# A hybrid attention step: a third score bank in turn, the first chunk in halves, and small pieces of work moved between engines

## The chip, the cores and the metric

The kernel runs on one core of a Trainium2 chip. TensorE (PE) multiplies, VectorE (DVE), ScalarE (ACT) and GpSimd (POOL) do the rest, and SyncE (SP) issues most transfers; each engine works through its own instructions in order. The metric is the time of one execution in microseconds (us).

## What is computed

One layer of a diffusion backbone on 128 context ("prompt") tokens and 1024 latent tokens, D = 1024. Cut to what matters:

```python
shift, scale, gate = split(silu(cond) @ w_mod + b_mod)
h = rmsnorm(x, norm_gain) * (1 + scale) + shift
q_a, k_a, v_a, g_a, q_b, k_b, v_b, g_b = split(h @ w_in)     # 8 heads and 2 kv heads of 64 in a and in b
q, k = rmsnorm(q), rmsnorm(k)                                # latent tokens: then a rotation by position
o_a = softmax(q_a k_a^T / 8) v_a                             # all latent keys and the cached context keys
o_b = softmax([sink, q_b k_b^T / 8]) v_b                     # keys within 128 positions, and the context keys
y = x + gate * (concat(o_a * silu(g_a), o_b * silu(g_b)) @ w_out)
```

The prompt attends to itself alone, and its keys and values are returned too.

## The kernel before

A float32 product is made of three products of rounded parts (high by high, low by high, high by low), so most operands exist twice, as a rounded "high" copy and a "low" rest. The rounded copies are casts, mostly on ScalarE; the rests are subtractions on VectorE or GpSimd. The kernel has these stages, and at the end of the program `in_order` fixes each engine's instructions to the order in which the Python code emitted them:

1. **Start and first gates** (0 to 66 us in the profile). Tokens come in nine tiles of 128 rows; tiles 1 to 8 are latent, tile 0 is the prompt. For each tile `squares` (L380 to L384) makes the inverse root mean square with ScalarE and GpSimd, `scaled` (L387) applies it on VectorE, `turned_tile` (L397) transposes the tile on TensorE in two banks (`px`, four 128x128 pieces each), and `keep` (L401) copies each bank into `xT`. For each chunk j of 128 model columns `modulate_rows` (L353) multiplies the conditioning with the scale and shift columns of `w_mod` (tile `wm`, loaded for j = 0 in two halves), a copy (L356, `mrows`), `modulate` (L362 to L368) turns that into columns `a_mod` and `b_col`, and `modulated` (L410 to L412) makes `h` (high on ScalarE, `hf` on VectorE, low on GpSimd). Then a loop over j multiplies chunk j-1 of `h` with the gate weights `W_GA` for tiles 1 to 4 (`pg_f`, L266 to L271, 512 columns), and chunk j-2 for tiles 5 and 6 (`pg_s`, 256 columns). `warm(n)` (L431) issues n products of the identity with itself into an unused bank; their result is never read.
2. **Queries, keys, values, second gates** (66 to 299 us). In the second gates the first output weights `wo` are split into high and low too (`split_wo`, L1043 and L1044).
3. **Attention and output** (299 us to the end). A unit i is (tile t, branch m, kv head g): i = 0 is tile 1, branch a, head 0; i = 1 the same in branch b; i = 2 branch a, head 1; and so on; units 32 to 35 are the prompt's. Every unit has *slots*, one for each block of 128 keys: nine in branch a, three or four in branch b. In a slot of branch a TensorE makes the scores `st` (L1170, L1171, two banks "B"), ScalarE their exponential `pe` (L1173) and its rounded copy `ph` (L1177), GpSimd the rest `pl` (L1181; block 4's on VectorE, L1179), and three slots later TensorE multiplies both with the values (`pv`, L1191 to L1194, two banks "C"). In branch b the scores `sn` (L944, L945) lie in banks "A" and are made while the branch-a unit before still runs, in its slots 0 to 3; VectorE masks them (L948), ScalarE makes the exponential `pen` (L934), and in the unit's own slots TensorE transposes it (L1165). The maxima of a later branch-a unit (`pmx` on TensorE, L889, `mx` on VectorE, L890) use banks "A" as well. When a unit's last values are done, `inverse` (L1203, or L1205 and L1206), `gated` (L1215, L1217) and `parts` (L1227, L1229) follow after `END_AT` = 1, 4, 6 slots, and after 9 its output products `po` (L1262) join a queue from which `OUTRATE` = 2.5 or `PADRATE` = 3 a slot are taken. The last five pieces of `wo` are loaded and split inside this stage: `WO_LATE` gives the slot of each load, the split comes three slots later.

The order in a slot is: what `tick` has due (casts, exponentials `pen`, subtractions), the scores, the loads, the maxima and branch-b scores, output products, and the values of three slots ago.

```python
BANKS = {"A": 2, "B": 2, "C": 2, "D": 1, "E": 1}
WO_LATE = {12: 13, 13: 20, 11: 27, 14: 29, 15: 31}
```

Bank "E" is used by transposes before the attention stage and by the output products there; the first of these take it after slot 24.

Of the kernel before, what the change touches and what calls it, by code (L numbers as in the profile page):

```python
# [115 lines left out]
def hybrid_step(ctx, tc, x_prompt, x_sample, cache_k_a, cache_v_a, cache_k_b, cache_v_b,  # L116
                cols, w_mod_ss, w_mod_g, b_mod, w_in, qn_a, kn_a, qn_b, kn_b, sink_b, w_out,
                k_ident, k_cos, k_sin, k_mask,
# [200 lines left out]
    with tc.tile_pool(name="st", bufs=2, side="right") as st:  # L319
        ident = st.tile([P, P], F32, name="ident", bufs=1)  # L320
        nc.sync.dma_start(ident, k_ident)
# [27 lines left out]
        def modulate_rows(j):  # L349
            pm = pmod[j] = bank_tr(f"pm{j}")  # L350
            for k in range(KT):
                a = 32 * (k % 4)
                nc.tensor.matmul(pm[a : a + 32, 0:256], sil32[:, k, :], wm[j][:, k].rearrange("p s n -> p (s n)"),  # L353
                                 start=(k < 4), stop=(k >= 4), tile_position=(0, a))
# [1 line left out]
            (nc.scalar.copy if j > 1 else nc.vector.tensor_copy)(mrows[j], pm[:, 0:256])  # L356
# [29 lines left out]
        def scaled(t):  # L386
            nc.vector.tensor_scalar(xn[t], xn[t], rx.pop(t), None, op0=ALU.mult)  # L387

        def turned_tile(t, tags, between=None):

            for c in range(2):
                if c and between:
                    between()
                px[t, c] = bank(tags[c], f"px{t}_{c}")
                for i in range(4):
                    k = 4 * c + i
                    nc.tensor.transpose(px[t, c][:, P * i : P * i + P], xn[t][:, P * k : P * k + P], ident)  # L397
# [5 lines left out]
        def modulated(j, t0, n, cond):  # L403
# [6 lines left out]
            nc.scalar.activation(h_at(0, i, j, to), xT[:, j, dst], AF.Identity, scale=a, bias=b)  # L410
# [998 lines left out]
```

## Time and profile before

| | us |
|---|---|
| median of 3 runs (lowest, highest) | 704.11 (703.66, 704.31) |
| the profiled execution | 703.62 |
| its span in the profile | 701.4 |
| busy in the span: PE, DVE, ACT, POOL | 690.6, 462.5, 419.2, 337.9 |

The profile is one execution. Its span runs from the first to the last instruction that was recorded; some 2 us lie around it. Rows of the timeline and of the chain of waits give the start in us from the span's start, the length, the engine, the line, and what is written and read. Matmuls overlap: a 128x512 one shows about 0.39 us, but the next starts 0.23 us after it. So two starts, not a length, tell what a product costs.

### The profile page before, as it was taken

How to read it: one execution, taken by the hardware profiler on the slowest of the kernel's cores; microseconds unless marked ns; L12 is line 12 of the kernel's file. 1: busy time of each engine (PE TensorE's matmuls, PEld its weight loads, DVE VectorE, ACT ScalarE, POOL GpSimd, SP SyncE). 2: the span in 40 equal slices, each digit the busy share in tenths (PEclk: the TensorE clock that was granted, in tenths of full speed). 3: DMA queues.
4: the chain of work that ended last, by engine and by line, in shares of the span. 5: the costliest groups of instructions: out<-in, count | busy, mean ns of one | idle time of the engine just before them, and what ended most of it. 6: DMA issues, size and time to landing. Idle time of an engine off the chain costs nothing.

```text
span 701.4 us, 10680 instructions
## 1 busy us (share of the span) xinstructions
PE 690.6 (98%) x3532; PEld 559.5 (80%) x3532; DVE 462.5 (66%) x998; ACT 419.2 (60%) x858; POOL 337.9 (48%) x358
## 2 busy tenths in 40 slices
PE   7999999999999999999999999999999999999997
PEld 4778988878788889986788787788887888887876
DVE  4667257968768854676667567567676775775563
ACT  6646411422313423399877887787788778877870
POOL 3547024233313321267676654765575557455752
PEclk9999999999999999999999999999999999999999
DMA  8962283349344016332222121122221221212324
GB/s 319 412 214 111 78 306 75 91 131 279 87 124 132 16 61 209 129 84 77 75 83 89 47 83 54 62 67 75 69 75 40 68 91 46 82 54 91 92 75 128
DMA packets 53703, 78.57 MB, mean 112 GB/s; under 512 B 7112, under 2 KB 25864, under 8 KB 52752
## 3 DMA queue, kind: packets, MB, share of 16 engines
q1 hardware_dynamic: 45952, 66.74, 28.9%
q10 hardware_dynamic: 7696, 11.15, 5.8%
q8 instruction: 28, 0.46, 0.3%
q14 instruction: 27, 0.22, 0.1%
HBM read 58.69 MB, written 19.18 MB: 111 GB/s over the span
## 4 chain that ended last, share of the span: by engine, by line
PE 94%; ACT 2%; DVE 2%; DMA 1%; issue 0%; POOL 0%; SPq 0%; ACTq 0%; DVEq 0%
PE po L1262 14%; PE pv L1191 7%; PE pv L1194 7%; PE pmx L889 5%; PE st L1170 5%; PE pv L1193 5%; PE pq L256 5%; PE pq L258 5%; PE st L1171 5%; PE pq L257 5%; PE st L1165 4%; PE pg L266 3%; PE pg L270 3%; PE pg L271 3%; PE pk L257 2%; PE pk L258 2%
## 5 line engine op out<-in xcount | busy, mean ns | idle before, releaser
L1181 POOL TENSOR_TENSOR pl<-pe,ph 128x512 fp32r<-128x512 f32 x130 | 167.8, 1293 | 142.7 <-DVE nm L948 64.4
L890 DVE TENSOR_REDUCE mx<-pmx 128x1 f32<-128x384 f32 x192 | 101.3, 552 | 58.5 <-PE pmx L889 56.0
L1173 ACT ACTIVATE pe<-st 128x512 f32<-128x512 f32 x146 | 86.8, 595 | 27.3 <-PE st L1171 26.5
L1177 ACT CAST ph<-pe 128x512 fp32r<-128x512 f32 x146 | 90.7, 621 | 4.8
L1191 PE MATMUL pv<-ph,v_hi 128*128 128x512 f32 x208 | 82.4, 396 | 0.1
L1194 PE MATMUL pv<-pl,v_hi 128*128 128x512 f32 x208 | 81.9, 394 | 0.0
L948 DVE CUSTOM_DVE_ANT_0 sn<-sn,mask,nsink 128x512 f32<-128x512 f32 (+1 forms) x64 | 46.3, 724 | 43.3 <-PE sn L945 39.2
L1262 PE MATMUL po<-wo,ogh 128*128 128x512 f32 (+1 forms) x224 | 73.2, 387 | 0.0
L181 POOL TENSOR_TENSOR rs_q<-ms_q,mhalf 128x8 f32<-128x8 f32 x18 | 34.1, 1896 | 80.9 <-DVE ms_q L179 80.9
L889 PE MATMUL pmx<-kha,qt 128*128 128x384 f32 x192 | 61.6, 365 | 1.1 <-ACT pen L934 0.8
L1170 PE MATMUL st<-qt,kha 128*128 128x512 f32 x144 | 57.7, 401 | 0.1
L1193 PE MATMUL pv<-ph,v_lo 128*64 128x512 f32 x146 | 57.7, 395 | 0.0
L1171 PE MATMUL st<-qb,kla 68*128 68x512 f32 x144 | 57.3, 398 | 0.0
L1194 PEld LDWEIGHTS pv<-pl,v_hi 128*128 128x128 f32 x208 | 39.0, 188 | 16.8
L934 ACT ACTIVATE pen<-sn,nm 128x512 f32<-128x512 f32 (+2 forms) x72 | 45.0, 626 | 5.7 <-DVE nm L948 2.3
L1166 ACT CAST ph<-st 128x512 fp32r<-128x512 f32 x62 | 36.4, 587 | 19.9 <-PE st L1165 19.6
L653 ACT CAST qo0q<-ptq 128x512 fp32r<-128x512 f32 x18 | 10.6, 586 | 60.4 <-PE ptq L650 58.8
L1262 PEld LDWEIGHTS po<-wo,ogh 128*128 128x128 f32 x224 | 41.0, 188 | 6.4
L1191 PEld LDWEIGHTS pv<-ph,v_hi 128*128 128x128 f32 x208 | 39.2, 189 | 7.8 <-issue 0.8
L1167 DVE TENSOR_TENSOR pl<-st,ph 128x512 fp32r<-128x512 f32 x62 | 42.6, 688 | 2.1 <-ACT ph L1166 1.4
L1262 PE MATMUL po<-wo,ogl 128*128 128x512 f32 (+1 forms) x112 | 43.5, 388 | 0.0
L889 PEld LDWEIGHTS pmx<-kha,qt 128*128 128x128 f32 x192 | 35.5, 190 | 7.3 <-DVE mx L890 1.8
(224 smaller groups left out, 1703.5 us busy)
## 6 DMA issues: line engine op xcount, KB each, us to landing
qt<-qd SPq DMA_DIRECT2D x36, 256.0 KB, 2.9
wm<-in_w_mod_ss_dram SPq DMA_DIRECT2D x7, 1024.0 KB, 9.7
qd<-qo0q ACTq DMA_DIRECT2D x36, 128.0 KB, 2.4
sgl<-gd SPq DMA_DIRECT2D x36, 128.0 KB, 2.3
out_dram<-yt SPq DMA_DIRECT2D x17, 256.0 KB, 2.1
xn<-in_x_sample_dram SPq DMA_DIRECT2D x8, 512.0 KB, 6.8
wg<-in_w_mod_g_dram SPq DMA_DIRECT2D x4, 1024.0 KB, 8.5
wraw<-in_w_out_dram SPq DMA_DIRECT2D x16, 256.0 KB, 4.5
```

What stands on the lines that cost most here:

```text
L257: nc.tensor.matmul(out, h_at(0, i, k, tok), w.lo[k], start=False, stop=False)
L889: nc.tensor.matmul(pm[:, 0:384], lhs, kha[:, g, 3 * b : 3 * b + 3, :], start=True, stop=True)
L890: nc.vector.tensor_reduce(mx[:, h, b : b + 1], pm[:, 0:384], axis=AX.X, op=ALU.max)
L1170: nc.tensor.matmul(s, kh, qtile[i], start=True, stop=False)
L1171: nc.tensor.matmul(s, kl, qbtile[i], start=False, stop=True)
L1173: nc.scalar.activation(pe, s, AF.Exp)
L1177: nc.scalar.copy(ph, pe)
L1181: nc.gpsimd.tensor_tensor(pl, pe, ph, op=ALU.subtract)
L1191: nc.tensor.matmul(pv, two, ph, start=(b == 0), stop=False)
L1193: nc.tensor.matmul(pv[0:64, :], vl, ph, start=False, stop=False)
L1194: nc.tensor.matmul(pv, two, pl, start=False, stop=last)
L1262: nc.tensor.matmul(po[c][:, at], a, wo_parts[KT * n + k][lo][:, at], start=(k == KS[0] and p == 0), stop=(k == KS[-1] and p == 2))
```

## The change

- **Start.** The identity is no longer loaded but made on GpSimd (`memset` and `affine_select`), and the small table `cols` is loaded from ScalarE's queue, so that SyncE's first transfer is tile 1. The first conditioning product is made in two halves of four k each. Tile 3's and tile 4's second transposes come after those of `modulate(0)`; tile 4 is scaled in two halves. ScalarE makes the first `b_col`, and the first chunk's high part `h` is made half by ScalarE and half by VectorE. There are 23 fillers of `warm` instead of 12: 14 ahead, 2, 2 and 1 between, 4 before the first gate product (as before).
- **First gates.** In the last round of the loop (j = 8) the small products of two of the four column groups come ahead of the big ones.
- **Second gates.** The low parts of `wo` pieces 0, 2, 4 and 6 are made on GpSimd instead of VectorE.
- **Attention.** Up to slot 24 the banks for `pmx`, `sn` and their small transposes go in turn A, A, E instead of A alone. Unit 1's copy `rs` goes from ScalarE to VectorE, unit 0's rounded `ogh` from ScalarE to GpSimd, and unit 0 is gated one slot earlier and split one slot later. The five late pieces of `wo` are loaded in slots 23, 24, 26, 28, 30 and so split in 26, 27, 29, 31, 33 (before: 16, 23, 30, 32, 34). In the fourth slot of the prompt (counted from unit 32's first as 0, number 3) one more output product is taken from the queue.

TensorE at the start, from the first transposes to the fillers ahead of the first gate product. `px_0` and `px_1` are the two banks of a tile, `xn_177` to `xn_183` are tiles 1 to 4 (in the kernel after: `xn_180` to `xn_186`), `pm` the conditioning product of chunk 0. Before:

```order
L397 MATMUL px_0_244<-ident,xn_177 128x128 x4
L397 MATMUL px_1_249<-ident,xn_177 128x128 x4
L397 MATMUL px_0_255<-ident,xn_179 128x128 x4
L397 MATMUL px_1_260<-ident,xn_179 128x128 x4
L397 MATMUL px_0_268<-ident,xn_181 128x128 x4
L397 MATMUL px_1_273<-ident,xn_181 128x128 x4
L353 MATMUL pm_281<-wm_185,sil_173 32x256 x8
L397 MATMUL px_0_299<-ident,xn_183 128x128 x4
L362 MATMUL pm_281<-ident,mrows_290 128x128 x2
L397 MATMUL px_1_310<-ident,xn_183 128x128 x4
```

After, from tile 2's second bank on:

```order
L419 MATMUL px_1_272<-ident,xn_182 128x128 x4
L462 LDWEIGHTS ident_b
L462 MATMUL idle<-ident_b 128x512
L462 LDWEIGHTS ident_b
L462 MATMUL idle<-ident_b 128x512
L371 MATMUL pm_283<-wm_188,sil_176 32x256 x4
L419 MATMUL px_0_288<-ident,xn_184 128x128 x4
L462 LDWEIGHTS ident_b
L462 MATMUL idle<-ident_b 128x512
L371 MATMUL pm_283<-wm_188,sil_176 32x256 x4
L419 MATMUL px_0_312<-ident,xn_186 128x128 x4
L382 MATMUL pm_283<-ident,mrows_303 128x128 x2
```

The first four of the eight products `pm` now stand ahead of tile 3's first bank, and tile 3's second bank has gone behind `modulate`'s two transposes.

ScalarE in unit 2's slots 2 to 5 (unit 2's first slot is slot 12 of the stage). Before:

```order
L1173 ACTIVATE pe_2_3647<-st_2_3642 128x512
L1177 CAST ph_2_3643<-pe_2_3647 128x512
L934 ACTIVATE pen_3609,sum_3611<-sn_2_3651,nm_3610 128x384
L1203 COPY rs_3662<-pv_3618 64x512
L1173 ACTIVATE pe_3_3669<-st_3_3664 128x512
L1177 CAST ph_3_3665<-pe_3_3669 128x512
L1043 CAST wo_big_3683<-wraw_3633 128x512
L934 ACTIVATE pen_3609,sum_3611<-sn_3_3673,nm_3610 128x384
L1173 ACTIVATE pe_4_3693<-st_4_3688 128x512
L1177 CAST ph_4_3689<-pe_4_3693 128x512
L1227 CAST ogh_3703<-spare 128x256
L1173 ACTIVATE pe_5_3714<-st_5_3709 128x512
```

After:

```order
L1217 ACTIVATE pe_2_3667<-st_2_3662 128x512
L1221 CAST ph_2_3663<-pe_2_3667 128x512
L978 ACTIVATE pen_3628,sum_3630<-sn_2_3671,nm_3629 128x384
L1217 ACTIVATE pe_3_3686<-st_3_3681 128x512
L1221 CAST ph_3_3682<-pe_3_3686 128x512
L978 ACTIVATE pen_3628,sum_3630<-sn_3_3690,nm_3629 128x384
L1217 ACTIVATE pe_4_3708<-st_4_3703 128x512
L1221 CAST ph_4_3704<-pe_4_3708 128x512
L1217 ACTIVATE pe_5_3724<-st_5_3719 128x512
```

Three instructions have left ScalarE here: the copy `rs`, the cast `wo_big` and the cast `ogh`.

GpSimd in the same unit, from block 5's rest on. Before:

```order
L1181 TENSOR_TENSOR pl_5_3711<-pe_5_3714,ph_5_3710 128x512
L1217 TENSOR_TENSOR spare<-spare,sgl_3357 128x256
L980 TENSOR_TENSOR sum_3611<-sum_3611,ex_3612 128x4
L1229 TENSOR_TENSOR ogl_3704<-spare,ogh_3703 128x256
L1181 TENSOR_TENSOR pl_6_3735<-pe_6_3738,ph_6_3734 128x512
L1181 TENSOR_TENSOR pl_7_3747<-pe_7_3750,ph_7_3746 128x512
```

After:

```order
L1225 TENSOR_TENSOR pl_5_3721<-pe_5_3724,ph_5_3720 128x512
L1271 CAST ogh_3737<-spare 128x256
L1261 TENSOR_TENSOR spare<-spare,sgl_3376 128x256
L1024 TENSOR_TENSOR sum_3630<-sum_3630,ex_3631 128x4
L1225 TENSOR_TENSOR pl_6_3747<-pe_6_3750,ph_6_3746 128x512
L1273 TENSOR_TENSOR ogl_3738<-spare,ogh_3737 128x256
L1225 TENSOR_TENSOR pl_7_3760<-pe_7_3763,ph_7_3759 128x512
```

The cast `ogh` has taken the place of the subtraction `ogl` ahead of block 6's rest, and `ogl` now stands ahead of block 7's.

The core of the diff:

```diff
-WO_LATE = {12: 13, 13: 20, 11: 27, 14: 29, 15: 31}
+SMALL_FIRST = 2
+LO_POOL = (0, 2, 4, 6)
+WO_LATE = {12: 23, 13: 24, 11: 26, 14: 28, 15: 30}
...
+RS_DVE = (1,)
+PHB_DVE = ()
+OG_POOL = (0,)
+AUX = ((24, "AAE"),)
-WARM = (8, 4)
+WARM = (14, 2, 2, 1, 4)
+ENDS = {0: (1, 3, 7, 9)}
+OUT_EXTRA = {3: 1.0}
...
+    aux_tags = ["A"]
+    def bank_aux(name):
+        turn["aux"] += 1
+        return bank(aux_tags[0][turn["aux"] % len(aux_tags[0])], name)
...
-        nc.sync.dma_start(ident, k_ident)
+        nc.gpsimd.memset(ident, 0.0)
+        nc.gpsimd.affine_select(ident, ident, pattern=[[-1, P]], compare_op=ALU.not_equal, fill=1.0, base=0,
+                                channel_multiplier=1)
-        nc.sync.dma_start(colt, cols)
+        nc.scalar.dma_start(colt, cols)
...
-            nc.vector.tensor_scalar(b_col[:, j, :], m4[:, 1], colt[:, 24 + j : 25 + j], None, op0=ALU.add)
+            if j == 0:
+                nc.scalar.activation(b_col[:, j, :], m4[:, 1], AF.Identity, bias=colt[:, 24 + j : 25 + j])
+            else:
+                nc.vector.tensor_scalar(b_col[:, j, :], m4[:, 1], colt[:, 24 + j : 25 + j], None, op0=ALU.add)
...
+            own = w // 2 if shared else w
+            nc.scalar.activation(h_at(0, i, j, slice(to.start, to.start + own)), xT[:, j, dst.start : dst.start + own],
+                                 AF.Identity, scale=a, bias=b)
+            if shared:
+                nc.vector.tensor_scalar(h_at(0, i, j, slice(to.start + own, to.stop)), xT[:, j, dst.start + own : dst.stop],
+                                        a, b, op0=ALU.mult, op1=ALU.add)
...
-        for t, tags in ((1, "AB"), (2, "AB"), (3, "CC")):
+        for t in (1, 2):
             scaled(t)
-            turned_tile(t, tags)
+            turned_tile(t, "AB")
+            warm(WARM[t])
...
-        scaled(4)
-        modulate_rows(0)
+        scaled(3)
+        modulate_rows(0, range(4))
+        turned_half(3, 0, "C")
+        warm(WARM[3])
+        for c in range(2):
+            keep(2, c, copies[c])
+        scaled(4, 2)
+        modulate_rows(0, range(4, KT))
         keep(3, 0, copies[0])
         W_GA.split(nc.gpsimd)
-        turned_tile(4, "AB", lambda: modulate(0))
+        turned_half(4, 0, "A")
+        modulate(0)
         keep(4, 0, copies[0])
-        modulated(0, 1, 4, 0)
+        turned_half(3, 1, "C")
+        turned_half(4, 1, "B")
+        modulated(0, 1, 4, 0, True)
...
+            if j == KT:
+                for ch in range(SMALL_FIRST):
+                    next_gates(ch, j - 2)
...
-            pm = bank("A", f"pmx{i}_{h}_{b}")
+            pm = bank_aux(f"pmx{i}_{h}_{b}")
...
-            s = bank("A", f"sn{i}_{h}")[:, 0:n]
+            s = bank_aux(f"sn{i}_{h}")[:, 0:n]
...
-        (nc.gpsimd if i in WO_LATE or i % 2 else nc.vector).tensor_tensor(lo, raw, hi, op=ALU.subtract)
+        (nc.gpsimd if i in WO_LATE or i % 2 or i in LO_POOL else nc.vector).tensor_tensor(lo, raw, hi, op=ALU.subtract)
...
-                nc.scalar.copy(v["rs"], pv[64:128, :])
+                (nc.vector.tensor_copy if i in RS_DVE else nc.scalar.copy)(v["rs"], pv[64:128, :])
...
-            nc.scalar.copy(oh, v["of"])
+            (nc.gpsimd.tensor_copy if i in OG_POOL else nc.scalar.copy)(oh, v["of"])
...
+        aux_tags[0] = next((tags for until, tags in AUX if s < until), "A")
...
         rate = OUTRATE if s < len(slots) and slots[s] else PADRATE
+        rate += OUT_EXTRA.get(s - start[32], 0.0)
```

More of the change, by code (lines that the diff above doesn't have):

```diff
@@ L146, in hybrid_step @@
     BANKS = {"A": 2, "B": 2, "C": 2, "D": 1, "E": 1}
-    turn = {"mm": 0, "tr": 0}
+    turn = {"mm": 0, "tr": 0, "aux": 0}
     mm_tags = ["BAAB"]
@@ L347, in hybrid_step, with modulate_rows @@
         mrows, pmod = {}, {}
-        def modulate_rows(j):
-            pm = pmod[j] = bank_tr(f"pm{j}")
-            for k in range(KT):
+        def modulate_rows(j, ks=range(KT)):
+            if 0 in ks:
+                pmod[j] = bank_tr(f"pm{j}")
+            pm = pmod[j]
+            for k in ks:
                 a = 32 * (k % 4)
@@ L354, in modulate_rows @@
                                  start=(k < 4), stop=(k >= 4), tile_position=(0, a))
+            if KT - 1 not in ks:
+                return
             mrows[j] = st.tile([P, 256], F32, tag="mrows", name=f"mrows{j}")
@@ L384, in squares, with scaled, turned_half, turned_tile @@
             nc.gpsimd.tensor_tensor(rx[t], ms, mhalf[:, 0:1], op=ALU.pow)
-        def scaled(t):
-            nc.vector.tensor_scalar(xn[t], xn[t], rx.pop(t), None, op0=ALU.mult)
-        def turned_tile(t, tags, between=None):
-            for c in range(2):
[L392 to L397, printed above, removed]
+        def scaled(t, parts=1):
+            r = rx.pop(t)
+            for p in range(parts):
+                half = xn[t][:, D // parts * p : D // parts * (p + 1)]
+                nc.vector.tensor_scalar(half, half, r, None, op0=ALU.mult)
+        def turned_half(t, c, tag):
+            px[t, c] = bank(tag, f"px{t}_{c}")
+            for i in range(4):
+                k = 4 * c + i
+                nc.tensor.transpose(px[t, c][:, P * i : P * i + P], xn[t][:, P * k : P * k + P], ident)
+        def turned_tile(t, tags):
+            for c in range(2):
+                turned_half(t, c, tags[c])
         def keep(t, c, copy):
@@ L468, in hybrid_step @@
         squares(5)
-        warm(WARM[1])
+        warm(WARM[4])
         big = [bank("AABB"[ch], f"pg0_{ch}_f") for ch in range(4)]
@@ L524, in hybrid_step @@
             for ch in range(4):
-                if small_on:
+                if small_on and not (j == KT and ch < SMALL_FIRST):
                     next_gates(ch, j - 2)
@@ L904, in transpose @@
         def transpose():
-            pt = bank("A", f"ptm{i}")
+            pt = bank_aux(f"ptm{i}")
             nc.tensor.transpose(pt[0:4, 0:P].bitcast(F32R), m_nat[i // 2 % 2], ident_r)
@@ L994, in turned @@
         def turned():
-            v["pt"] = bank("A", f"pti{i}")[0:4, 0:P]
+            v["pt"] = bank_aux(f"pti{i}")[0:4, 0:P]
             nc.tensor.transpose(v["pt"], v["inv"], ident_r.bitcast(F32))
@@ L1165, in scores @@
                 nc.tensor.transpose(s[:, P * h : P * h + P], penat[i][:, h, o : o + P], ident_r.bitcast(F32))
-            nc.scalar.copy(ph, s)
+            (nc.vector.tensor_copy if (i, b) in PHB_DVE else nc.scalar.copy)(ph, s)
             later(1, lambda: nc.vector.tensor_tensor(pl, s, ph, op=ALU.subtract))
```

8 lines of the change are left out of this document (3 added, 5 removed).

## Prediction

> **What bounds the kernel now.** I read the page's busy table and chain first. The page's rows:
>
> ```profile
> span 701.4 us, 10680 instructions
> PE 690.6 (98%) x3532; PEld 559.5 (80%) x3532; DVE 462.5 (66%) x998; ACT 419.2 (60%) x858; POOL 337.9 (48%) x358
> PE 94%; ACT 2%; DVE 2%; DMA 1%; issue 0%; POOL 0%; SPq 0%; ACTq 0%; DVEq 0%
> ```
>
> TensorE is busy nearly all the time and holds 94% of the chain. No product is taken out here, so only time in which TensorE waits can be won. Next, the table of its waits (first the line that waited, then the releaser, total, times, longest):
>
> ```profile
> PE idle L431 <- DVE ident_b L323: 3.4, 1, 3.4
> PE px L397 <- DVE xn L387: 1.2, 1, 1.2
> PE pmx L889 <- ACT pen L934: 0.8, 1, 0.8
> ```
>
> The largest is the wait for the first filler, the next that for the first transpose; a bank that ScalarE frees too late follows. As a matmul's shown length exceeds its cost, short stalls hide in this table, so I also compared starts. Four places came out: the start, 60 us, 316 to 333 us, 674 us. The change touches all four.
>
> **The start.** The chain of waits up to the first gate product, cut, and the timeline there:
>
> ```profile
> 2.58 6.36 DMA xn<-in_x_sample_dram
> ...
> 13.04 1.00 PE pm L353 x16
> ...
> 14.63 0.41 PE pm L362 x2
> ...
> 15.28 0.39 DVE a_mod L366
> ...
> 15.89 0.82 ACT h L410
> 16.76 0.50 PE pg_f L270
> ```
>
> ```profile
> 0.72 0.40 SPq L321 DMA_DIRECT2D ident<-in_k_ident_dram  x1
> 1.64 1.85 SPq L375 DMA_DIRECT2D xn<-in_x_sample_dram  x4
> 3.38 3.60 PE L431 MATMUL idle<-ident_b 128*128 128x512 bf16 x8 [3.38 <-DVE ident_b L323]
> 13.68 0.62 ACT L241 CAST whiga<-rawga 128x512 fp32r<-128x512 f32 x1 [0.45 <-DMA rawga<-in_w_in_dram]
> 14.11 0.42 DVE L356 COPY mrows<-pm 128x256 f32<-128x256 f32 x1 [0.75 <-PE pm L353]
> 14.67 0.59 ACT L401 COPY xT<-px 128x512 f32<-128x512 f32 x1 [0.37 <-PE px L397]
> 15.30 1.03 PE L431 MATMUL idle<-ident_b 128*128 128x512 bf16 x4
> ```
>
> Before, `pm` stood behind tile 3's transposes, which waited for tile 3's transfer (landed 8.94), its squares and its scaling. After, TensorE meets half of `pm` ahead of tile 3, and the rest needs only the second half of `wm`. That lies in the queue just ahead of `rawga`, 256 KB which landed at 13.68; at the stretch's 346 GB/s (row below) `wm` was complete some 0.7 earlier, at about 13.0. Tile 1's transfer is now SyncE's first, at 0.72 instead of 1.64, 0.92 earlier, and with it every transfer behind it: `wm` 12.1. The second half of `pm` (half of 1.00) ends about 12.75, `mrows` (0.42 and some 0.1 of passing on) 13.3, the two transposes 13.7, the reduction 14.0. `a_mod` 0.39 and ScalarE's `b_col`, which takes the place of VectorE's, bring 14.5. ScalarE has one copy of `xT` (0.59) in the way, say to 14.85. The half `h` costs about half of 0.82 on either engine: 15.4. TensorE's own work there, tile 3's and 4's second banks and four fillers (0.59, 0.60, 1.03), fits by 15.4 too. So the first gate product comes at about 15.45 instead of 16.76: **−1.3**. Bounds: −0.5 if only the halved `h` counts (0.4 and passing on), −1.8 if `xT`'s copy isn't in the way and the lead is whole.
>
> ```profile
> 8.17:13.00 4.83, 4.72 (x28) 4.16 (x28) 3.27 (x5) 3.73 (x7) 2.25 (x5) 1.00 0.99 346
> ```
>
> The making of the identity is an unshown operation. The nearest are three of POOL's groups (total, mean ns): the power that a root uses, a subtraction, and a product with one input.
>
> ```profile
> L181 POOL TENSOR_TENSOR rs_q<-ms_q,mhalf 128x8 f32<-128x8 f32 x18 | 34.1, 1896 | 80.9 <-DVE ms_q L179 80.9
> L1229 POOL TENSOR_TENSOR ogl<-spare,ogh 128x256 fp32r<-128x256 f32 x36 | 26.4, 735 | 0.0
> L733 POOL TENSOR_SCALAR v_hi<-gain 128x256 fp32r<-128x256 f32 x5 | 2.0, 402 | 0.0
> ```
>
> By the last, 128 columns take 0.2, by the subtraction 0.37, by the power, 1.90 for 8, 0.24 a column and so 30. `affine_select` has one input and plain comparisons, so I take 0.4, beside the cheap rows; the other end stays for the range. The bf16 copy follows at about 1.5 (its loaded one let the first filler go at 3.38). Fourteen fillers of 0.42 (eight show 3.60, less what the last one's length overhangs) take 5.9, to 7.4 or so; tile 1's transposes could start at 7.25, as the first stood at 8.17:
>
> ```profile
> 8.17 4.88 PE L397 MATMUL px<-ident,xn 128*128 128x128 f32 x24 [1.19 <-DVE xn L387]
> ```
>
> Some 0.7 is spare on that way, since of the 4.88 the transposes themselves need less and TensorE waits for `wm` until 12.1. So the identity is **free** up to some 1.1 us of `affine_select`, and the fillers with it.
>
> The eight fillers ahead ran at about 0.42 each, the four at 15.30 at about 0.22 (1.03 less the overhang): TensorE's speed doubled in between, though the granted clock of the windows row (the 1.00) shows nothing of it. The Trainium skill, "TensorE: Matmul & The Clock Gate", section "What's actually happening", says that TensorE runs at half speed until a free-running window of some 3.4 us has been busy. By it, fillers of 5.9 us surely hold one whole window only if it began late enough, two windows being 6.8; the rows bear out the two speeds, but not where a window ends. By the page the sum stays where the window falls well, and else becomes that of the third rival below.
>
> **The small gate products.** The timeline at 60 us:
>
> ```profile
> 60.32 0.40 PE L271 MATMUL pg_f<-h,wloga 128*128 128x512 f32 x1
> 60.88 0.73 PE L266 MATMUL pg_f<-h,whiga 128*128 128x512 f32 x2 [0.16 <-POOL h L412]
> ```
>
> The starts lie 0.56 apart instead of 0.23: 0.33 lost, on POOL's low rest of the last chunk. Two groups of small products now stand ahead and cover more than that: **−0.33** (0 if their own operand, of POOL too, is late).
>
> **Low parts of `wo`.** POOL stood idle there for 23 us:
>
> ```profile
> 276.10 1.29 POOL L1044 TENSOR_TENSOR wo<-wraw,wo 128x512 fp32r<-128x512 f32 x1 [23.29 <-ACT wo L1043]
> ```
>
> Four subtractions of 1.29 fit into this; VectorE is relieved of them, which TensorE feels at most as one short stall: **0** (−0.2 to +0.2).
>
> **Attention, 316 to 333 us.** Windows (TensorE busy first, then weight loads, VectorE, ScalarE, POOL), the chain, and ScalarE's and POOL's rows:
>
> ```profile
> 316.32:332.75 16.43, 14.90 (x60) 9.80 (x60) 10.04 (x24) 15.55 (x33) 12.20 (x13) 1.00 0.24 75
> ```
>
> ```profile
> 323.13 0.58 ACT rs L1203
> ...
> 324.90 0.61 ACT wo_big L1043
> ...
> 326.14 0.44 PE pmx L889
> ...
> 331.14 0.57 DVE mx L890
> ```
>
> ```profile
> 327.13 0.40 ACT L1227 CAST ogh<-spare 128x256 fp32r<-128x256 f32 x1
> 328.75 1.29 POOL L1181 TENSOR_TENSOR pl<-pe,ph 128x512 fp32r<-128x512 f32 x1 [0.37 <-ACT ph L1177]
> ...
> 331.70 3.77 POOL L1181 TENSOR_TENSOR pl<-pe,ph 128x512 fp32r<-128x512 f32 x3
> ```
>
> ScalarE has 15.55 of work in 16.43: it is the bound here. TensorE's 60 matmuls, at 0.23 a start for 512 columns and 0.175 for 384, with its transposes come to about 12.4, so some 4.0 are lost, in two ways. Until 326.14, `pmx` waits for a bank A which `sn` holds until ScalarE's `pen` has read it, and `pen` stands behind `rs` and `wo_big`. From there to 332.75 are 6.61, in which TensorE has 18 products of 0.23 and 6 `pmx` of 0.175, 5.2: the other 1.4 go where `pmx` waits for VectorE's `mx` to free one of the two banks A, as at 331.14.
>
> The copies and casts that leave ScalarE are 0.58 + 0.61 + 0.40, or 1.44 from start to start. `rs` and `wo_big` lie ahead of block 3's `pen`, which by my replay ends 1.2 earlier (324.9, where `pmx` at 326.14 shows it at 326.1): −1.2. The third bank lets `pmx` go on while `mx` reads: −1.4. `rs` costs VectorE the same 0.58, in a stretch where it has 10.04 of work in 16.43. What is late next is POOL, which takes over `ogh`. The one-input row of that shape has 0.40, the two-input rows 0.74; I take 0.40. From block 5's rest, about 1.5 earlier than 328.75, POOL owes 1.29 + 0.40 + 0.74 + 1.29 and a small sum, to about 331.1, then `ogl` and block 7's rest, to 333.1, and TensorE would want them some 0.4 before: +0.4. Together **−2.2**; bounds −0.8 (half of the ScalarE time, the bank without effect, as POOL's row of three rests without a gap binds instead) and −3.0 (the bank's and ScalarE's part, and POOL's debt mostly hidden).
>
> **Slots 24 to 35.** Two splits of `wo` that stood in slots 16 and 23 now stand in 26 and 27, and all five come every one or two slots: 2 x 0.61 more on ScalarE (the `wo_big` above) and 2 x 1.29 more on POOL there, on thin cover:
>
> ```profile
> 346.96 0.19 ACT L934 ACTIVATION_READ_ACCUMULATOR pen<-sn,nm 128x1 f32 x1
> 348.31 0.52 PE L889 MATMUL pmx<-kha,qt 128*128 128x384 f32 x2
> ```
>
> `pen` is done at 347.15, 1.16 ahead of the `pmx` that follows it, which two casts would use up if both fell ahead of one `pen`; their slots differ. So it is covered but for a rest, and I charge **+0.2** (0, to +0.6 if half of one POOL subtraction lies uncovered before a product).
>
> **The product in the prompt.** At the first prompt values:
>
> ```profile
> 673.67 0.84 DVE L1215 TENSOR_TENSOR spare<-pv,rs 64x256 f32<-64x256 f32 x2
> 674.11 0.40 PE L1262 MATMUL po<-wo,ogh 128*128 128x512 f32 x1
> 674.66 0.47 PE L1191 MATMUL pv<-ph,v_hi 128*128 128x512 f32 x1
> ```
>
> `pv` needs a bank C that VectorE reads until 674.51; TensorE starts 0.55 after the last product, 0.32 more than one costs. One product of 0.23 now fills it: **−0.23** (0 if the product is missed later in the queue).
>
> **Sum.** −1.3 − 0.33 + 0 − 2.2 + 0.2 − 0.23 = −3.86. From the profiled execution, 703.62, this gives **699.8**. The median of before, 704.11, lies 0.49 above that execution, and a median of new runs may lie as much above the sum; the range holds it.
>
> **Rivals.**
> - *Attention stays bound by ScalarE and POOL.* ScalarE's 15.55 is for it, of which only 1.44 leaves, and so is POOL's 3.77 (three rests without a gap). Against it is the 0.8 wait for a bank in the table of waits. The gain there is 0.8 instead of 2.2: **701.2**.
> - *The lead at the start isn't kept.* For it: from 8 to 13 us the transfers run at 346 GB/s and a share of 0.99, so an earlier issue may only queue. Against it: what is queued ahead is the same or less. Then only the halved `h` and the order remain, between 0 and −0.5, and the start gives 0.3 instead of 1.3: **700.8**.
> - *TensorE is still slow at the transposes.* Gaps between the fillers could cause it. The second half of `pm` (0.5), the two transposes (0.41) and the four fillers (1.03) lie on the way to the first gate product, and double; with 0.3 for transposes queued ahead, 2.2 are lost against the forecast: **702.0**. Against it: the clock was up by then before, with fewer fillers.
> - *Slower: the identity is late.* All of TensorE's first work needs it. If `affine_select` costs by the column as the power row does, at 0.19 to 0.24 for each of 128, it takes 24 at least. It costs from 1.1 on, cancels the whole gain (3.9) at 5.0, and at 24 makes 703.6 + 24 − 5.0 = **722.6**. For it: POOL's rows per column differ more than a hundredfold. Against it: only the power is dear, its plain operations are not.
>
> **How the numbers follow.** Chances: the forecast 0.63 (for itself 698.4 to 701.0), attention bound 0.14, lead not kept 0.12, slow transposes 0.07, identity late 0.04. The range's low end is the forecast with its better bounds in part (start −1.8, attention −3.0, slots 0, so 1.5 less, and −0.2 for the low parts and the product at 60 us with more cover, weighed as unlikely all at once): **697.9**. Its high end is the slow transposes' 702.0 with 0.3 of the 0.49 that the median lay higher: **702.3**. A measurement of this kernel can tell about 0.2%, 1.4 us, from no change. Faster by more means below 702.7: the forecast, attention bound and lead not kept nearly whole, and some of the slow transposes, **0.88**. Within it, two rivals together or the slow transposes with the late slots, **0.07**. Slower, the late identity and 0.01 for a stall that it shares a place with, **0.05**.
>
> **What would show it.** Right: the first `pg_f` between 15.2 and 15.8; tile 1's transfer issued near 0.7; no 0.3 gap at 60 us; slot 24 near 335.3 instead of 337.6 from the same origin, no `pmx` waiting on `pen`; `ogh` on POOL near 0.4; no gap ahead of `pv` at the prompt. Wrong: a first filler after 4 us; rows of POOL's rests that TensorE waits for in slots 20 to 30; a `pmx` or `st` that waits on ScalarE behind `wo_big`.

## The result, and the profile after

| | before | after |
|---|---|---|
| median (lowest, highest), 6 runs each, side by side | 704.15 (703.66, 704.31) | 699.81 (699.69, 699.94) |
| the profiled execution | 703.62 | 699.82 |
| its span | 701.4 | 697.7 |

The ratio is 0.9939, with a 95% interval of 0.9926 to 0.9952. The prediction was 699.8, in a range of 697.9 to 702.3. A sum can be right by errors that cancel, so each of its terms is looked at below.

The page after, its busy table and the chain's shares:

```profile
span 697.7 us, 10706 instructions
PE 690.7 (99%) x3543; PEld 558.9 (80%) x3543; DVE 460.6 (66%) x996; ACT 418.6 (60%) x857; POOL 343.5 (49%) x365
PE 97%; DMA 1%; ACT 1%; issue 0%; DVE 0%; POOL 0%; SPq 0%; POOLq 0%; ACTq 0%
```

TensorE works as long as before, 690.7 for 690.6; only its waits went. Its table of waits after:

```profile
PE idle L462 <- DVE ident_b L339: 2.0, 1, 2.0
PE pm L371 <- DMA wm<-in_w_mod_ss_dram: 0.5, 2, 0.4
PE pmx L933 <- ACT pen L978: 0.3, 1, 0.3
```

The wait for `pen` has shrunk from 0.8 to 0.3, and a new one has come in: `pm`, at the start, waits for the transfer of `wm`.

Where the time went is read by taking the same TensorE product in both traces and subtracting its starts. The difference stands still between the places at which something was won or lost:

| TensorE product, start before | start after minus start before | what this stretch won (forecast) |
|---|---|---|
| first gate product, 16.76 | −1.66 | |
| tile transposes, 32.95 | −1.25 | start −1.25 (−1.3) |
| second gates, 65.86 | −1.78 | 60 us −0.53 (−0.33) |
| first `sn` of unit 3, 316.80 | −2.01 | low parts −0.23 (0) |
| transposes of unit 5, 357.09 | −3.84 | attention −1.83 (−2.2) |
| the next ones, 358.51 | −3.58 | later slots +0.26 (+0.2) |
| last products, 691.17 | −3.73 | prompt −0.15 (−0.23) |
| end of the span, 701.45 | −3.77 | |

Now the places. The start, in the timeline after:

```profile
0.99 0.29 POOL L336 TENSOR_SCALAR_AFFINE_SELECT ident<-ident 128x128 f32<-128x128 f32 x1
2.03 5.25 PE L462 MATMUL idle<-ident_b 128*128 128x512 bf16 x14 [2.03 <-DVE ident_b L339]
7.29 1.09 PE L419 MATMUL px<-ident,xn 128*128 128x128 f32 x8
15.10 0.47 PE L284 MATMUL pg_f<-h,whiga 128*128 128x512 f32 x1
16.62 1.07 PE L371 MATMUL pm<-wm,sil 128*32 128x256 f32 x16 [0.35 <-DMA wm<-in_w_mod_ss_dram]
22.30 0.62 ACT L255 CAST whiga<-rawga 128x512 fp32r<-128x512 f32 x1 [1.02 <-DMA rawga<-in_w_in_dram]
```

`affine_select` took 0.29, so the identity was in time. The first gate product came at 15.10, before the forecast's 15.45; but chunk 1's `pm` then waited for its weights, and some six microseconds later ScalarE's cast waited for `rawga`, where neither had waited before. In the profile before, these rows read:

```profile
17.89 0.42 PE L353 MATMUL pm<-wm,sil 128*32 128x256 f32 x4
```

```profile
22.55 0.62 ACT L241 CAST whiga<-rawga 128x512 fp32r<-128x512 f32 x1
```

The stretch of the attention stage that was 316.32 to 332.75 before, in the windows view after (length, then TensorE, weight loads, VectorE, ScalarE, POOL, granted clock):

```profile
314.32:328.90 14.58, 14.11 (x60) 9.94 (x60) 9.87 (x24) 13.78 (x30) 10.21 (x12) 1.00 0.19 57
```

It is 1.85 shorter; ScalarE lost three instructions and 1.77 of work. Two rows of POOL there, and two at 354 us:

```profile
326.45 0.39 POOL L1271 CAST ogh<-spare 128x256 fp32r<-128x256 f32 x1
```

```profile
351.91 1.27 POOL L1088 TENSOR_TENSOR wo_big<-wraw,wo_big 128x512 fp32r<-128x512 f32 x1
353.15 2.53 POOL L1225 TENSOR_TENSOR pl<-pe,ph 128x512 fp32r<-128x512 f32 x2
```

```profile
354.10 0.39 PE L1237 MATMUL pv<-ph,v_lo 128*64 128x512 f32 x1
354.48 0.50 PE L1238 MATMUL pv<-pl,v_hi 128*128 128x512 f32 x1
354.82 0.60 PE L1209 MATMUL st<-ident_r,pen 128*128 128x128 f32 x4
```

The cast `ogh` costs POOL the 0.39 that was taken for it. At 354 us `pv` starts 0.38 after its neighbour instead of 0.23, and the next row 0.34 after it: POOL finishes the first of the two `pl` at 354.4, as `wo_big`'s low part stands ahead of it. This is the price of the later splits.

### The profile page after: what moved, and what is told of

The parts are those of the page before. It is cut to its first block, busy times and chain, and to the rows that moved or that the text cites. A ratio compares the mean times of both kernels' runs of the same rounds, so it can differ in the third digit from the quotient of the medians.

```text
span 697.7 us, 10706 instructions
## 1 busy us (share of the span) xinstructions
PE 690.7 (99%) x3543; PEld 558.9 (80%) x3543; DVE 460.6 (66%) x996; ACT 418.6 (60%) x857; POOL 343.5 (49%) x365
## 4 chain that ended last, share of the span: by engine, by line
PE 97%; DMA 1%; ACT 1%; issue 0%; DVE 0%; POOL 0%; SPq 0%; POOLq 0%; ACTq 0%
PE po L1306 14%; PE pv L1235 7%; PE pv L1238 7%; PE pmx L933 5%; PE st L1214 5%; PE pv L1237 5%; PE pq L272 5%; PE st L1215 5%; PE pq L270 5%; PE pq L271 5%; PE st L1209 4%; PE pg L284 3%; PE pg L280 3%; PE pg L285 3%; PE pk L271 2%; PE pk L272 2%
```

## The experiments

Eleven runs were made, in three groups; each kernel of a group stood beside the kernel before on one chip. Parts that act far apart in the program were put into one kernel, since the comparison of starts reads each by itself. The table gives starts minus those of the kernel before, all from profiles; the text quotes from it.

| kernel | chunk 1's `pm`, 17.89 | 32.95 | 65.86 | 291.31 | 316.80 | 357.09 | 358.51 | 691.17 | median us (lowest, highest) |
|---|---|---|---|---|---|---|---|---|---|
| changed | −1.27 | −1.25 | −1.78 | −1.99 | −2.01 | −3.84 | −3.58 | −3.73 | 699.81 (699.69, 699.94) |
| three_undone | −1.64 | −1.33 | −1.33 | −1.02 | −1.03 | −3.22 | −2.97 | −2.95 | 700.20 (699.76, 700.64) |
| bank_undone | −1.67 | −1.69 | −2.21 | −2.43 | −2.44 | −3.65 | −3.41 | −3.58 | 700.47 (699.98, 700.98) |
| scalar_undone | −0.80 | −0.56 | −1.08 | −1.30 | −1.30 | −0.70 | −0.70 | −0.85 | 702.03 (701.60, 702.83) |
| bank_ident_alone | −1.05 | −1.07 | −1.06 | −0.55 | −0.55 | −0.89 | −0.89 | −0.96 | 702.95 (702.35, 704.79) |
| changed_again | −1.17 | −1.13 | −1.66 | −1.87 | −1.88 | −3.72 | −3.45 | −3.61 | 699.61 (699.38, 699.94) |
| splits_undone | −1.51 | −1.48 | −2.00 | −2.21 | −2.22 | −3.33 | −3.33 | −3.49 | 700.40 (700.07, 700.81) |
| fillers_rs | −0.20 | −0.24 | −0.76 | −0.97 | −0.98 | −2.31 | −2.06 | −2.25 | 700.10 (699.81, 701.15) |
| lo14_wm1 | −1.88 | −1.55 | −2.09 | −2.30 | −2.31 | −3.21 | −3.20 | −3.36 | 700.00 (699.91, 700.82) |
| ident_fillers14 | −1.48 | −0.75 | −0.73 | −0.69 | −0.68 | −0.40 | −0.40 | −0.47 | 703.03 (702.81, 703.25) |
| late14_wm1 | −1.63 | −1.55 | −2.09 | −2.31 | −2.33 | −4.19 | −4.19 | −4.35 | 699.09 (698.85, 699.91) |
| changed_third | −1.62 | −1.41 | −1.93 | −2.16 | −2.18 | −4.01 | −3.76 | −4.02 | 699.69 (699.53, 700.00) |

The kernel before had medians of 704.08, 703.99 and 704.06 in the three groups. All rows are taken against its one profile. The three profiles of the changed kernel differ by up to 0.45 at `pm` and by 0.28 at 32.95, so differences of that size at the start are scatter; what they win in the attention stage is 1.83, 1.84 and 1.83.

### Three small parts undone

```diff
-SMALL_FIRST = 2
+SMALL_FIRST = 0
-LO_POOL = (0, 2, 4, 6)
+LO_POOL = ()
-OUT_EXTRA = {3: 1.0}
+OUT_EXTRA = {}
```

> The changed kernel with three parts undone that lie far apart: the small gate products in their old place, the low parts of the even wo pieces on VectorE again, no extra output product in the prompt. Read each by the start of the same TensorE product in both traces. By the changed trace: TensorE falls 0.53 us behind the changed kernel at the last first gates (65 us), another 0.27 at 276 us, another 0.2 at 674 us: some 1.0 in all, 700.8 us. By the prediction's terms: 0.33, 0 and 0.23, 0.56 in all, 700.4 us.

The gain at 60 us is gone (0.00 between 32.95 and 65.86, 0.53 with it), and so is that in the prompt. The low parts cost 0.31 instead of winning 0.21, and at another place than expected:

```profile
282.31 0.22 PE L950 MATMUL ptm<-ident_r,m_nat 128*4 128x128 f32 x1 [0.36 <-DVE mx L934]
```

TensorE waits for the maxima on VectorE, and these stand behind a low part that took 1.63, while one on POOL, begun 0.21 ahead of it, was running. In ident_fillers14, which makes these low parts on VectorE too, VectorE's began first, took 0.69, and TensorE lost only 0.05 from 65.86 to 316.80; there POOL's was the longer one. First the rows of three_undone, then those of ident_fillers14:

```profile
279.95 1.29 POOL L1088 TENSOR_TENSOR wo<-wraw,wo 128x512 fp32r<-128x512 f32 x1 [2.16 <-ACT wo L1087]
280.16 1.63 DVE L1088 TENSOR_TENSOR wo<-wraw,wo 128x512 fp32r<-128x512 f32 x1
```

```profile
281.02 0.69 DVE L1046 TENSOR_TENSOR wo<-wraw,wo 128x512 fp32r<-128x512 f32 x1
281.36 1.50 POOL L1046 TENSOR_TENSOR wo<-wraw,wo 128x512 fp32r<-128x512 f32 x1 [2.96 <-ACT wo L1045]
```

So what relieving VectorE is worth depends on how the two subtractions meet: 0.5 beside this run, 0.2 against the kernel before. The time, 700.20 with a ratio of 0.9947 (0.9932 to 0.9962), overlaps with the changed kernel's; its start happened to be 0.37 earlier at `pm`. Its places decide, not its time.

### The bank undone, and the first `h` whole

```diff
-AUX = ((24, "AAE"),)
+AUX = ()
-        modulated(0, 1, 4, 0, True)
+        modulated(0, 1, 4, 0)
```

> The changed kernel with the banks A alone again in the attention stage (316 us on), and, at the start, the first chunk's high part whole on ScalarE. Start: if the transfer of chunk 1's modulation weights is what bounds, the first gate product comes some 0.25 us later, but from chunk 1's conditioning product on nothing is lost (0.0); by the prediction's sum, in which the halves are worth 0.4, 0.25 to 0.4 us stay lost. Attention: by the prediction (1.2 from ScalarE, 1.4 from the bank, 0.4 given back) the bank's loss is 1.4 us or a little less, 0.5 to 0.8 of the measured 1.85 staying; if the bank alone carries the stage, all of the 1.85 but 0.1 is lost; if ScalarE's relief carries it, under 0.5 is lost. Times: 701.2, 701.6, 700.2 us.

Attention still wins 1.21 (−2.44 to −3.65) without the bank; the bank is worth 0.62 of 1.83, not 1.4. Its waits for a bank are back:

```profile
317.31 0.45 PE L988 MATMUL sn<-khb,qt 128*128 128x384 f32 x1 [0.24 <-ACT pen L978]
319.02 0.45 PE L988 MATMUL sn<-khb,qt 128*128 128x384 f32 x1 [0.15 <-ACT pen L978]
328.10 0.45 PE L933 MATMUL pmx<-kha,qt 128*128 128x384 f32 x1 [0.18 <-DVE mx L934]
```

The first two cost nothing in the end: at the `pmx` that was 326.14 before, both kernels have won 1.25 (changed −3.26 from −2.01, bank_undone −3.70 from −2.44), for there ScalarE's `pen` sets the pace with either number of banks. All of the bank's 0.62 comes behind it. From there to the end of the stretch are 6.02 in the changed kernel, against 6.61 before and 5.2 of TensorE's own. Most of the rest is VectorE:

```profile
327.09 1.27 PE L933 MATMUL pmx<-kha,qt 128*128 128x384 f32 x3
```

```profile
326.84 2.42 DVE L934 TENSOR_REDUCE mx<-pmx 128x1 f32<-128x384 f32 x5
```

Five maxima in the changed kernel follow each other without a gap there, 0.48 each, and `pmx` can run ahead of them by one bank more, not faster than they do: the three `pmx` start 0.36 and 0.46 apart instead of 0.18, some 0.5 in all. At the start nothing was lost by the whole `h`: the first gate product came at 15.09, and `pm` was even earlier. ScalarE's `h`, first in the changed kernel, then here:

```profile
14.41 0.60 ACT L437 ACTIVATE h<-xT,b_col,a_mod 128x256 fp32r<-128x256 f32 x1
```

```profile
14.22 0.81 ACT L437 ACTIVATE h<-xT,b_col,a_mod 128x512 fp32r<-128x512 f32 x1
```

The half saves 0.2, not the forecast's 0.4, and as the path ahead of it was 0.2 earlier in this profile, the two gate products coincide.

### ScalarE's relief undone, and the identity loaded again

```diff
-RS_DVE = (1,)
-OG_POOL = (0,)
-ENDS = {0: (1, 3, 7, 9)}
-WO_LATE = {12: 23, 13: 24, 11: 26, 14: 28, 15: 30}
+RS_DVE = ()
+OG_POOL = ()
+ENDS = {}
+WO_LATE = {12: 13, 13: 20, 11: 27, 14: 29, 15: 31}
...
-        nc.gpsimd.memset(ident, 0.0)
-        nc.gpsimd.affine_select(ident, ident, pattern=[[-1, P]], compare_op=ALU.not_equal, fill=1.0, base=0,
-                                channel_multiplier=1)
+        nc.sync.dma_start(ident, k_ident)
...
-        nc.scalar.dma_start(colt, cols)
+        nc.sync.dma_start(colt, cols)
```

> The changed kernel with the copy rs, the cast ogh and the late output weights back where they were (unit 0's ends too), the third bank kept; and, at the start, the identity and the small table loaded by SyncE ahead of tile 1 again. Start: if transfers bound it, the whole 0.92 us of lead goes; if the order and the halves are what counts, 0.0 to 0.3; if the 14 fillers, which now begin near 3.4 us, delay the transposes, over 1.3. Attention: by the prediction 1.2 us less the 0.4 given back is lost, 0.8, and the 0.26 us stall at block 7's values of slot 33 goes, so 0.5 at the end; if the bank alone carries the stage, under 0.1; if ScalarE becomes the bound as soon as the bank lets TensorE go ahead, 1.4. Times with a start of +0.92: 701.2, 700.5, 701.9 us.

The start lost 0.69 of its 1.25 at 32.95, three quarters of the lead's 0.92. Attention lost more than any theory gave: it is 0.60 slower than before, 2.43 slower than changed. The windows around it show why (TensorE first, the granted clock is the value behind POOL's):

```profile
322.00:325.39 3.39, 1.71 (x7) 0.85 (x6) 0.42 (x1) 3.31 (x8) 3.39 (x4) 1.00 0.02 6
325.39:328.72 3.33, 3.33 (x9) 2.34 (x9) 2.41 (x5) 3.23 (x8) 2.94 (x4) 0.51 0.40 119
```

For 3.33 us the granted clock was 0.51, and eight products started 0.42 to 0.43 apart instead of 0.23, some 1.5 us. Its four runs with a mean clock of 0.998 took 702.29 to 702.83, the four with 0.999 or 1.000 took 701.60 to 701.77. So part of the loss is not the wait but what the wait did to the clock. The medians of the two groups lie 0.74 apart; only the slower one has a trace.

### The bank and the identity alone, in the kernel before

```diff
+AUX = ((24, "AAE"),)
...
+        nc.gpsimd.memset(ident, 0.0)
+        nc.gpsimd.affine_select(ident, ident, pattern=[[-1, P]], compare_op=ALU.not_equal, fill=1.0, base=0,
+                                channel_multiplier=1)
-        nc.sync.dma_start(ident, k_ident)
...
+        nc.scalar.dma_start(colt, cols)
-        nc.sync.dma_start(colt, cols)
```

> The kernel before with two parts of the change alone: the third bank in the attention stage, and, at the start, the identity made on GpSimd and the small table on ScalarE's queue. Start: if transfers bound it, this alone wins the lead of 0.9 us (first gate product near 15.9), and no more; by the prediction, in which the order of conditioning product and tile 3 is what frees the path, 0.5 to 0.9. Attention: by the prediction 1.4 us; if the bank alone carries the stage, 1.8; if both parts are needed, under 0.9. Times: 701.8, 701.4, 702.3 us.

The lead alone gives 1.07 at 32.95, most of the start's 1.25. The bank alone gives 0.34 (−0.55 to −0.89), under the 0.9 named for "both parts are needed". But this is a loss and a gain. At the `pmx` that was 326.14 before it had lost 0.28 (−0.27), and so had ident_fillers14, whose attention stage is that of before (−0.68 to −0.39), by arriving at another moment. Behind it the bank won 0.62 here, and ident_fillers14 won 0.01. So the bank is worth the same 0.6 without ScalarE's relief: the two parts end different waits, and their gains add up. The ten runs scatter from 702.35 to 704.79. Four of them, with a mean clock of 0.995, took 703.29 to 703.85; of the others one took 704.79 and five 702.35 to 702.61. Between 65.86 and 291.31 it lost 0.51, at the same wait of `ptm` as above, behind a low part of 1.73.

### The late splits undone, and chunk 1's weights first

```diff
-WO_LATE = {12: 23, 13: 24, 11: 26, 14: 28, 15: 30}
+WO_LATE = {12: 13, 13: 20, 11: 27, 14: 29, 15: 31}
...
-        load_x(5)
         load_wm(1)
+        load_x(5)
```

> The changed kernel with the five late output weights back in their old slots alone (rs, ogh and the third bank stay), and, at the start, chunk 1's modulation weights issued ahead of tile 5. Attention: the cast wo_big stands ahead of a pen again; by the prediction's reading (ScalarE's instructions ahead of pen count one to one) 0.5 to 0.6 us is lost between 316 and 333 us, and the 0.26 us wait at 354 us goes: 0.3 lost. If the bank hides it, 0.26 is won. If TensorE's speed drops after the longer waits, as in the run with all of ScalarE's work put back, 1.5 and more is lost. Start: if the transfer bounds chunk 1's product, it begins 0.3 to 0.4 earlier, at about 16.2; if not, nothing.

Attention wins 1.11 instead of 1.83: `wo_big` ahead of `pen` costs 0.72, and undoing it takes the 0.26 at 354 us away (0.00 between 357.09 and 358.51). Together a net loss of 0.46, a little more than one to one. Chunk 1's `pm` began at 16.38, without a wait.

### The copies undone, and the old fillers

```diff
-RS_DVE = (1,)
-OG_POOL = (0,)
-WARM = (14, 2, 2, 1, 4)
-ENDS = {0: (1, 3, 7, 9)}
+RS_DVE = ()
+OG_POOL = ()
+WARM = (8, 0, 0, 0, 4)
+ENDS = {}
```

> The changed kernel with the copy rs back on ScalarE, the cast ogh too, unit 0's ends as before (the late splits and the bank stay as changed); and, at the start, only the 8 fillers ahead and the 4 behind of the kernel before. Attention: one to one ahead of pen, 0.5 to 0.6 us is lost for rs, 0 to 0.4 for ogh, which stands behind it; if only the sum of ScalarE's work counts, 0.9; if TensorE's speed drops, 1.5 or more. Start: if transfers bound it, the first gate product comes up to 0.6 later but chunk 1's product no more than 0.1 later; if the fillers are what carries the start, both come 0.6 or more later.

Attention wins 1.33 instead of 1.83: `rs` and `ogh` are worth 0.50. At the `pmx` that was 326.14 before, 0.72 had been lost, more than one to one for `rs`; 0.22 of it came back behind. With the 0.72 for the splits the 0.50 makes 1.22, about what bank_undone kept. The start was the surprise: of 1.25 only 0.24 stayed in this profile. TensorE there:

```profile
7.56 3.68 PE L419 MATMUL px<-ident,xn 128*128 128x128 f32 x16 [1.95 <-DVE xn L413]
11.17 1.08 PE L371 MATMUL pm<-wm,sil 128*32 128x256 f32 x8
12.18 1.12 PE L419 MATMUL px<-ident,xn 128*128 128x128 f32 x4
13.23 0.64 PE L371 MATMUL pm<-wm,sil 128*32 128x256 f32 x8
13.80 0.66 PE L419 MATMUL px<-ident,xn 128*128 128x128 f32 x4
```

Sixteen transposes took 3.68, where eight took 1.09 in the changed kernel: TensorE was at half speed until 13.2 (four transposes 1.12, then 0.66), and on the path. This profile was the longest of its runs, 701.15; the other three, of which there is no trace, took 699.81 to 700.12, so it may not start like this every time.

### A first try to beat both

```diff
-        (nc.gpsimd if i in WO_LATE or i % 2 or i in LO_POOL else nc.vector).tensor_tensor(lo, raw, hi, op=ALU.subtract)
+        (nc.gpsimd if i != 14 and (i in WO_LATE or i % 2 or i in LO_POOL) else nc.vector).tensor_tensor(lo, raw, hi, op=ALU.subtract)
...
-        load_x(5)
         load_wm(1)
+        load_x(5)
```

> A version meant to beat both: the changed kernel with the low part of output weight 14 made on VectorE, which is idle at 352 us, instead of GpSimd, which works there without a gap from 342 to 357 us; and chunk 1's modulation weights issued ahead of tile 5. By the traces the 0.26 us wait at 354 us goes, and the wait of chunk 1's product shrinks by up to 0.35: 699.2 us. If the first wait only moves to VectorE's maxima, and the second to tile 5 or to the next weights, nothing: 699.8 us.

The wait at 354 us went, and a larger one came at 350. VectorE's rows:

```profile
348.92 1.13 DVE L1088 TENSOR_TENSOR wo_big<-wraw,wo_big 128x512 fp32r<-128x512 f32 x1 [0.98 <-ACT wo_big L1087]
349.97 2.10 DVE L934 TENSOR_REDUCE mx<-pmx 128x1 f32<-128x384 f32 x4
```

The subtraction waited 0.98 for ScalarE's cast, with four `mx` queued behind it, and TensorE lost 0.98 (−4.19 at 332.75, read as in the table, to −3.21). VectorE's idle time was not where the subtraction had to stand.

### Identity and fillers alone

```diff
+        nc.gpsimd.memset(ident, 0.0)
+        nc.gpsimd.affine_select(ident, ident, pattern=[[-1, P]], compare_op=ALU.not_equal, fill=1.0, base=0,
+                                channel_multiplier=1)
-        nc.sync.dma_start(ident, k_ident)
...
+        nc.scalar.dma_start(colt, cols)
-        nc.sync.dma_start(colt, cols)
...
-WARM = (8, 4)
+WARM = (14, 4)
```

> The kernel before with the identity made on GpSimd, the small table on ScalarE's queue, and 14 fillers ahead instead of 8; order, halves, attention and all else as before. If transfers and TensorE's speed are all that bounds the start, the first gate product comes near 15.4 us and chunk 1's conditioning product at 16.3 to 16.6, as in the changed kernel, 1.3 to 1.6 before the old 17.89, and less scatter than the run with 8 fillers had (702.35 to 704.79 with the bank): 702.6 us. If the new order and the halves are needed for it, chunk 1's product stays near 16.84, as with 8 fillers: 703.0 us.

With the old order and whole `h` the first gate product came at 15.28 and `pm` at 16.41, as in the changed kernel: the new order isn't needed for that. By 32.95 half of it was given back, at the next transfer:

```profile
22.95 0.62 ACT L241 CAST whiga<-rawga 128x512 fp32r<-128x512 f32 x1 [1.91 <-DMA rawga<-in_w_in_dram]
```

The eleven runs lie within 702.81 to 703.25, against 702.35 to 704.79 with 8 fillers and the bank. Whether the fillers or the missing bank narrowed them, these runs don't separate.

### A second try to beat both

```diff
-WO_LATE = {12: 23, 13: 24, 11: 26, 14: 28, 15: 30}
+WO_LATE = {12: 23, 13: 24, 11: 26, 14: 29, 15: 31}
...
-        load_x(5)
         load_wm(1)
+        load_x(5)
```

> A version meant to beat both: the changed kernel with the splits of the output weights 14 and 15 in slots 32 and 34, as in the kernel before, so that GpSimd makes block 7's rest ahead of weight 14's, and chunk 1's modulation weights issued ahead of tile 5. By the traces the 0.26 us wait at 354 us goes and some 0.2 to 0.3 of the start's with it: 699.2 us beside the changed kernel on the same chip at 699.6. If GpSimd's gapless stretch only makes another rest late, or the start's wait moves to the next weights, nothing.

> The changed kernel, for comparison with the version meant to beat it on the same chip: 699.4 to 699.9 us, chunk 1's product between 16.2 and 16.7 us.

The splits of 14 and 15 one slot later put block 7's rest ahead of weight 14's. The wait is gone (0.00 between 357.09 and 358.51; `pv`, `pv` and the transposes start 0.23 and 0.24 apart):

```profile
353.75 0.40 PE L1237 MATMUL pv<-ph,v_lo 128*64 128x512 f32 x1
353.98 0.39 PE L1238 MATMUL pv<-pl,v_hi 128*128 128x512 f32 x1
354.22 0.60 PE L1209 MATMUL st<-ident_r,pen 128*128 128x128 f32 x4
```

It took 699.09, 0.9933 of before (0.9919 to 0.9946); the changed kernel on the same chip took 699.69, 0.9938 (0.9926 to 0.9951). The intervals overlap. By the places the 0.25 at 354 us is sure. The weights' order gives 0.14 at 32.95 against changed_third, less than the scatter of that place.

### The changed kernel again

> The changed kernel once more, beside the next ones. Chunk 1's conditioning product began at 16.62 us in its first profile and at 16.2 in two kernels that differ from it elsewhere; if that is the transfer's own scatter, it lies anywhere from 16.2 to 16.6 here, and the time with it, 699.4 to 699.9 us; if it was the kernel, it is 16.6 again.

Chunk 1's `pm` began at 16.72, in changed_third at 16.27: it is the transfers' scatter. Attention won 1.84 and 1.83, the later slots lost 0.27 and 0.25; it is mainly the start that moves from run to run.

## Why the prediction was right

The time was right: −3.86 forecast, −3.77 measured at the end of the span. That it came so near is partly luck, since the terms below miss by up to 0.4, in both directions. The bound was right in the main: what was won were TensorE's waits at the four places, and some 0.2 at a fifth, in the second gates. Term by term:

- **Start, −1.3 forecast, −1.25 measured.** The size was right and the path only partly. The lead of 0.92 was there, and the lead alone gave 1.07. But the prediction's sum walked the path to the first gate product and stopped there. That path was 0.35 shorter than worked out (the second half of `pm` began at 11.87, where the sum had its weights at 12.1), and the end of it doesn't count: chunk 1's `wm` and the next `rawga` bind next. The half `h`, for which the sum took half of 0.82, took 0.60; the halves moved nothing behind it (bank_undone), and the old order with 14 fillers reached the same `pm` (ident_fillers14), though it lost more at `rawga`. How much of the 0.38 to 0.66 by which the changed kernel was ahead of it in its three profiles at 32.95 belongs to the order, and how much to the scatter of that transfer, wasn't tried.
- **Fillers, nothing forecast.** As a cost that is right; as a worth it isn't: without the eleven additional ones a profile lost 1.0 at 32.95, though the other three runs of that kernel were 1.0 to 1.3 shorter. The rival "TensorE is still slow at the transposes" had the right mechanism. What was held against it, that the clock was up by then before, with fewer fillers, was wrong. In the kernel before sixteen transposes fill 3.53 us, and only the next eight run at full speed:

```profile
8.17:11.70 3.53, 3.53 (x16) 3.27 (x16) 2.00 (x3) 2.52 (x5) 1.46 (x4) 1.00 0.97 323
```

```profile
11.95 1.09 PE L397 MATMUL px<-ident,xn 128*128 128x128 f32 x8
```

In each of the three traces with eight fillers ahead (the kernel before, bank_ident_alone, fillers_rs) 11 to 16 of the first transposes start some 0.21 after the one before; in the ten with fourteen ahead, none does. So the fillers are what kept the rival from happening.
- **60 us, −0.33 forecast, −0.53 measured.** One gap was read, 0.56 between two starts. Beside it stand 0.32 at 59.53 and 0.34 at 60.88 where 0.23 is the rule: 0.09 + 0.33 + 0.11 = 0.53. All three are in the timeline before; the first is this:

```profile
59.53 0.48 PE L270 MATMUL pg_f<-h,whiga 128*128 128x512 f32 x1
59.85 0.40 PE L271 MATMUL pg_f<-h,wloga 128*128 128x512 f32 x1
```

- **Low parts, 0 forecast, −0.23 measured** (with its neighbours, from 65.86 to 316.80). The better end that was named, −0.2, was it. Undone, they cost 0.52: the prediction counted VectorE's work and not how its subtraction meets POOL's.
- **Attention, −2.2 forecast, −1.83 measured.** ScalarE's 1.2 was right: 1.21 without the bank, and 0.50 + 0.72 by its parts. The bank's 1.4 was the step that failed: 0.62. The prediction read all of TensorE's 1.4 of waiting behind 326 us as a lack of banks; a third bank took 0.6 of it. Of the other 0.8 some 0.5 is the pace of VectorE's five `mx`, which no bank quickens; the rest lies where a product follows a `pmx` by 0.26 to 0.28, for which 0.175 was taken. The 0.4 to be given back to POOL didn't appear: `ogh` cost 0.39, as taken, but TensorE never waited for `ogl` or the rests there. Errors of 0.8 and 0.4, of opposite sign, left 0.4.
- **Later slots, +0.2 forecast, +0.26 measured,** but not at `pen`, whose row was quoted: it was the POOL subtraction ahead of a rest, named as the bound of +0.6.
- **Prompt, −0.23 forecast, −0.15 to −0.26 measured** in three runs of the changed kernel.

Of the rivals, "attention stays bound by ScalarE and POOL" gave 0.8 for that stage, less than half of the 1.83; the lead of "the lead isn't kept" was kept by itself, 1.05 at `pm` and 1.07 at 32.95; and "the identity is late" is settled by one row of 0.29.

## What to carry to other kernels

Where a chain of waits is shortened, follow it to the next transfer behind its end: what lies beyond that transfer's arrival isn't won. A wait that two resources cause isn't the sum of both; taking one away shows what the other still holds, and only undoing each by itself gives their shares. And before work is moved to an engine with idle time, look at what the moved instruction would wait for, and at what is queued behind it.
